# A hybrid SSD, GLA and attention layer step: loading each weight block in two steps

## The chip, the cores and the metric

One core of a Trainium2 chip runs the whole program in one launch. The metric is the device time of one execution in microseconds, as the median of several runs; lower is better.

## The reference, cut to what matters

The reference runs two layers over a context sequence of 128 tokens and a latent sequence of 2048 tokens. Each layer normalises its input, projects it with one wide matrix, runs three groups of heads on the result and projects back:

```python
shift, scale, gate = modulation(c, w_ada, b_ada)
h = rms_norm(x, norm_w) * (1 + scale[:, None]) + shift[:, None]
z, xbc, dt, gq, gk, gv, gg, glr, aq, ak, av, ag = split_proj(h @ w_in)
y_ssd, _ = ssd_branch(z, xbc, dt, conv_w, conv_b, a_log, dt_bias, d_skip, ssd_norm_w, ssd_h0)
y_gla, _ = gla_branch(gq, gk, gv, gg, glr, gk_up, gk_b, gla_norm_w, gla_s0)
y_att = latent_attention(qh, kh, vh, k_ctx, v_ctx, sink) * jax.nn.silu(ag)
y = jnp.concatenate([y_ssd, y_gla, y_att], axis=-1) @ w_out
return x + gate[:, None] * y
```

`w_in` is 1024 x 3120 and `w_out` 1024 x 1024 for each layer, in float32.

## The kernel before, in words

**Tiles and stages.** The tokens are 17 tiles of 128 rows: 16 latent tiles and one context tile (CT). The normalised input of all tiles stays on the chip, transposed, as two float16 halves (a value and what rounding left over) in the tile `HT`. Each layer runs in stages: GLA's chunked scan in groups of two tiles (A), attention tile by tile (T) with the outputs of GLA between, the SSD's convolution and scan (S), and the output projection (O), which also normalises the next layer's input. Every projection is the function `prod` (L276 to L282): 24 float16 matmuls that add three products of halves for each of the eight blocks of 128 input columns.

**Loading weights.** A block of 256 columns of `w_in` or `w_out` is 1 MB in float32 and goes to one of nine slots (ring at L227, `slot` at L229). `load_w` (L233 to L271) makes 34 such loads, 17 for each layer. It

- issues the transfer from SyncE's (SP's) queue (L241);
- squares the block on ScalarE (ACT) with a sum along each row into `amx` (L246, or L252 in six pieces for `w_out`); the squares themselves are thrown away into the shared buffer `upper`;
- adds these sums over the partitions with a 128x1 matmul on TensorE (PE), `all_sum` (L219 to L223), whose result is a PSUM tile of tag "m";
- makes a power of two of it in seven small VectorE (DVE) operations (`pow2_scale`, L188 to L204), scales and rounds the block into `upper` on ACT (L257, L263), takes the rest on DVE into the slot (L258, L264) and copies the rounded half from `upper` into the slot (L265).

There is one `upper` for all loads, so the next load's squares wait until L265 has read the one before. The loads of a layer stand in the list `todo` (L292, L293) in the order wqk, wv, wdl, waq, wakv, wag, wgg, wx0 to wx3, wz0, wz1, wo0 to wo3; `upto(n)` makes those up to the n-th. It is called between the stages' steps: three loads at the start of the program; one after each of several GLA groups (L1283, L1285, L1428); at L1357 before GLA's outputs; after the attention tiles 1, 4, 7, 13 and 15 (L1387 to L1389); after the SSD groups 1 to 3 (L1407), and once before the output stage (L1408). The three first loads of layer 1 come during layer 0's output stage (L1422, L1426).

**PSUM.** Its eight banks are given out by tag: "d" has two, "s" four and "m" two (L147). Projections mostly take "d" and "s". "m" serves `all_sum`, `all_max`, transposes, the modulation (L365), GLA's products (L596, L616), attention's values (L892) and the states (L1033).

**The order of the work.** The kernel is written as one long program; a planner, built into the language, orders the instructions of each engine from their places in the program and a plan of when their inputs are ready, so on each engine the order can differ from the text, but each engine runs its own list in order, waiting wherever an input is late.

**Start of the program.** The modulation's rows for the latent tiles go through DRAM (L416, read back by L456). The context tile is transposed by PE (`normalise`, L446); a latent tile is normalised on DVE (L461, L462), split (L463 on ACT, L464 on DVE) and transposed by a DMA (L466). Layer 1's modulation weights come by transfers from GpSimd's (POOL's) queue (L350).

Of the kernel before, what the change touches and what calls it, by code (L numbers as in the profile page):

```python
# [14 lines left out]
AF = mybir.ActivationFunctionType  # L15
ALU = mybir.AluOpType
# [4 lines left out]
P = 128  # L21
# [57 lines left out]
def hybrid_kernel(ctx, tc, a, o):  # L79
# [139 lines left out]
    def all_sum(src):  # L219

        pr = psum()
        T.matmul(pr[:, 0:1], lhsT=ones, rhs=src, start=True, stop=True)
        return pr[:, 0:1]  # L223
# [5 lines left out]
    def slot():  # L229
        ring.append(ring.pop(0))  # L230
        return slots[ring[-1]]

    def load_w(src, l, ranges, name, dst=None, row_scale=None):  # L233
        n = sum(y - x for x, y in ranges)
        raw = slot() if dst is None else dst
        st = view(raw, [P, KB, n])
        w = view(raw, [P, 2, KB, n], F16)
        hi = view(upper, [P, KB, n], F16)
        off = 0
        for x, y in ranges:  # L240
            D.dma_start(st[:, :, off:off + y - x], src[l, :, x:y].rearrange("(k p) c -> p k c", p=P))  # L241
            off += y - x

        amx = sb("wmx", [P, 1])
        if row_scale is None:
            S.activation(hi.bitcast(BF16), st, AF.Square, accum_out=amx)  # L246
        else:

            blocks = [slice(k, k + 1) for k in range(4)] + [slice(4, 6), slice(6, 8)]
            part = sb("wmp", [P, 6])  # L250
            for i, ks in enumerate(blocks):
                S.activation(hi[:, ks].bitcast(BF16), st[:, ks], AF.Square, scale=row_scale[:, i:i + 1], accum_out=part[:, i:i + 1])  # L252
            V.tensor_reduce(amx, part, AX.X, ALU.add)
        c, ci = pow2_scale(all_sum(amx), "w", True)

        if row_scale is None:
            S.activation(hi, st, AF.Copy, scale=c)  # L257
            V.scalar_tensor_tensor(w[:, 0], st, c, hi, ALU.mult, ALU.subtract)  # L258
        else:
            cg = sb("wcg", [P, 6])  # L260
            V.tensor_scalar(cg, row_scale, c, None, ALU.mult)
            for i, ks in enumerate(blocks):
                S.activation(hi[:, ks], st[:, ks], AF.Copy, scale=cg[:, i:i + 1])  # L263
                V.scalar_tensor_tensor(w[:, 0, ks], st[:, ks], cg[:, i:i + 1], hi[:, ks], ALU.mult, ALU.subtract)  # L264
        V.tensor_copy(w[:, 1], hi)  # L265
        inv = sb(name + "i", [P, 1])
        if row_scale is None:
            V.tensor_tensor(inv, ci, hinv[l], ALU.mult)
        else:
            V.tensor_copy(inv, ci)  # L270
        return w[:, ::-1], inv  # L271

    def load_in(l, *ranges, name, dst=None):
        return load_w(a["w_in"], l, ranges, name, dst)
# [210 lines left out]
            s.wg, s.ig = load_in(l, (2064, 2320), name="wgg")  # L485

    def gla_begin(l, s, order):

        s.inc = 0 if order == sorted(order) else 1
        s.order = order  # L490
        s.iq = sb("giq", [P, 1])
        V.tensor_scalar(s.iq, s.iqk, 32.0 ** -0.5, None, ALU.mult)
        s.up = sb("ups", [P, P])
        for d in range(2):
            D.dma_start(s.up[32 * d:32 * d + 16], a["gla_gk_up"][l, d])
            D.dma_start(s.up[32 * d + 16:32 * d + 17], a["gla_gk_b"][l, d:d + 1])

        s.sx, s.dec = k_gla
        V.memset(s.sx[:, 0, 1], 0.0)
        V.memset(s.sx[:, 1, 2], 0.0)  # L500
        s.ent = sb("ent", [P, 4, 64])
        e = 0 if s.inc == 0 else 2 * len(GROUPS[order[0]]) - 1
        D.dma_start(s.ent[:, e], a["state_gla"][0, l, s.inc].rearrange("h k v -> (h k) v"))
        s.lr = [sb("lr", [P, 2, 64]) for i in range(2)]
        for x in s.lr:
            G.memset(x, 1.0)
        s.am = [sb("am", [P, 4, 2, 64]) for i in range(2)]
        s.at = [sb("at", [P, 4, 64]) for i in range(2)]
        for x in s.am:
            G.memset(x, 0.0)  # L510
        dt_raw[l] = k_dtraw
# [150 lines left out]
        D.dma_start(o["new_state_gla"][0, l, 1].rearrange("h k v -> (h k) v"), s.sx[:, 1, 0])  # L662

    def gla_out_begin(l, s):
        s.igh = sb("ggh", [P, 1])
        V.tensor_scalar(s.igh, s.ig, 0.5, None, ALU.mult)
        s.bd = [sb("bd", [P, 2, 2, P]) for i in range(1)]
        for x in s.bd:
            G.memset(x, 0.0)
# [66 lines left out]
            s.wg, s.ig = load_in(l, (2864, 3120), name="wag")  # L736

    def att_begin(l, s):
        s.sca, s.nw, s.sink, s.vc, s.kct, s.isc = k_att
        s.igh = sb("aigh", [P, 1])  # L740
        s.pts = [[sb(f"pts{kv}", [P, 1024]) for kv in range(2)], halves(slot())]
        V.tensor_scalar(s.igh, s.ig, 0.5, None, ALU.mult)
        for hh in range(6):
            src = a["attn_q_norm"] if hh < 4 else a["attn_k_norm"]
            D.dma_start(s.nw[:, hh], src[l:l + 1, :].to_broadcast([P, 64]))
        D.dma_start(s.sink, a["attn_sink"][l:l + 1, :].to_broadcast([P, 4]))

        kc = sb("asq", [P, 2, 64])
        D.dma_start(kc, a["cache_k"][0, l])
        vc = sb("qkx", [P, P])  # L750
        D.dma_start(vc, a["cache_v"][0, l].rearrange("s h d -> s (h d)"))

        mw = sb("mw", [P, 2])
        V.tensor_reduce(mw[:, 0:1], s.nw[:, 0], AX.X, ALU.max, apply_absolute_value=True)
        V.tensor_reduce(mw[:, 1:2], s.nw[:, 4], AX.X, ALU.max, apply_absolute_value=True)
        V.tensor_scalar(mw, mw, 12.0, None, ALU.mult)
        mk = sb("tmx", [P, 1])
        V.tensor_reduce(mk, kc, AX.XY, ALU.max, apply_absolute_value=True)
        V.tensor_tensor(mw[:, 1:2], mw[:, 1:2], all_max(mk), ALU.max)
        cq, iq = pow2_scale(mw[:, 0:1], "t")  # L760
        ck, ik = pow2_scale(mw[:, 1:2], "t")
        V.tensor_scalar(s.nw[:, 0:4], s.nw[:, 0:4], cq, None, ALU.mult)
        V.tensor_scalar(s.nw[:, 4:6], s.nw[:, 4:6], ck, None, ALU.mult)
        V.tensor_copy(s.isc[:, 1:2], ik)
        V.scalar_tensor_tensor(s.isc[:, 0:1], iq, 0.125, ik, ALU.mult, ALU.mult)
        V.tensor_scalar(kc, kc, ck, None, ALU.mult)
        x16 = sb("x16", [P, 1024], F16)
        split_keys(x16, kc)
        D.dma_start_transpose(out=s.kct, in_=x16[:, 512:1024])

        mv = sb("tmx", [P, 1])
        V.tensor_reduce(mv, vc, AX.X, ALU.max, apply_absolute_value=True)
        bv = sb("abv", [P, 1])
        V.tensor_scalar(bv, s.ikv, hnorm[l], None, ALU.mult)
        V.tensor_tensor(bv, bv, all_max(mv), ALU.max)
        cv, iv = pow2_scale(bv, "t")
        s.vs, s.igv = s.sca[:, 0:1], s.sca[:, 1:2]
        V.tensor_tensor(s.vs, s.ikv, cv, ALU.mult)
        V.tensor_tensor(s.igv, s.igh, iv, ALU.mult)
        split(s.vc, vc, cv)  # L780
        s.qt, s.kt, s.v, s.pt, s.rl = {}, {}, {}, {}, {}
# [216 lines left out]
        s.w.append(w)  # L998

    def ssd_begin(l, s):  # L1000
        s.Z = arena(sb("SS", [P, where["SS"][2]]))

        s.sl, s.at = [[s.Z([P, P], BF16) for d in range(2)] for i in range(2)], [s.Z([P, P], BF16) for i in range(2)]
        s.sr = [s.Z([P, 8, P], BF16) for i in range(2)]
        for x in s.at:
            G.memset(x, 1.0)

        for x in s.sl:
            for d in range(2):
                G.memset(x[d], 0.0)  # L1010
                G.memset(x[d][64 * d:64 * d + 32], 1.0)
        D.dma_start(s.dsk, a["ssd_d"][l:l + 1].to_broadcast([P, 8]))
        s.wx, s.cw = [], []
        for j in range(4):
            w, iw = s.w[j]
            s.wx.append(w)

            cw = s.Z([P, 5, 2])
            V.tensor_scalar(cw, vec[l][:, 0:40].rearrange("p (j b) -> p j b", b=8)[:, :, 2 * j:2 * j + 2], iw, 0.5, ALU.mult, ALU.mult)
            s.cw.append(cw)  # L1020
        s.cbias = s.Z([P, 8])
        V.tensor_scalar(s.cbias, vec[l][:, 40:48], 0.5, None, ALU.mult)
        s.h, s.accs = {}, {}
        for d in range(2):
            ssd_enter(l, s, d, "s0")
# [132 lines left out]


    def out_begin(l, s):  # L1160
        s.wz, s.izh = [], []
        for j in range(2):
            w, iz = s.w[4 + j]
            izh = sb(f"izh{j}", [P, 1])
            V.tensor_scalar(izh, iz, 0.5, None, ALU.mult)
            s.wz.append(w)
            s.izh.append(izh)
        s.wo, s.io = zip(*s.w[6:10])

        s.rows = halves(slot())  # L1170
# [119 lines left out]
    def loads(l, gla, att, ssd):  # L1290
# [2 lines left out]
        todo += [(ssd_load, ssd, i) for i in range(10)]  # L1293

        def upto(n):
            while len(todo) > 17 - n:
                f, s, i = todo.pop(0)
                f(l, s, i)
# [165 lines left out]
```

## Time and profile before

| | |
|---|---|
| median of three runs | 2300.2 us (2296.73 to 2302.02) |
| profiled execution | 2304.28 us |
| its span | 2302.5 us, 53686 instructions |
| mean granted TensorE clock | 0.959 of full speed |

The span is the time from the first to the last instruction of the profiled execution; times of day in the rows below are microseconds from its start. PE is a matmul, PEld its weight load.

### The profile page before, as it was taken

The numbers are of one execution on the slowest core, as the hardware profiler recorded it, in microseconds if no ns is written. First come the engines' busy times: TensorE is split into PE (matmuls) and PEld (weight loads), VectorE is DVE, ScalarE is ACT, GpSimd is POOL, SyncE is SP. The second block draws the span as 40 slices with busy tenths as digits, with TensorE's granted clock in tenths as the row PEclk, the third lists the DMA queues.
The fourth block names the chain that finished last, engine by engine and source line by source line (L and its number), as shares of the span: only waits on it lengthen the run. The fifth ranks groups of instructions, "written<-read, shape, count | busy, mean of one in ns | idle before, by whom it ended". The sixth has DMA issues, their size and how long they took to land. (4 is left out here: it accounts for less than half of the span.)

```text
span 2302.5 us, 53686 instructions
## 1 busy us (share of the span) xinstructions
PE 2080.7 (90%) x21228; PEld 1750.4 (76%) x21245; DVE 1628.4 (71%) x4088; ACT 992.4 (43%) x2185; POOL 878.6 (38%) x918
## 2 busy tenths in 40 slices
PE   2596888999899899998999999899999999989998
PEld 0364767778688788887888887777888778878887
DVE  2465768887599988666665657898779988854442
ACT  2333554665444434433333554666563433422221
POOL 0010015556434354544442003566643344444442
PEclk6797979999899999999999999999999999999999
DMA  8687434576710112676667123556751101265553
GB/s 298 165 263 158 121 103 92 124 154 143 168 58 33 38 38 91 183 199 163 168 160 201 41 69 100 122 125 149 160 139 43 38 33 42 81 182 164 154 146 96
DMA packets 486352, 288.01 MB, mean 125 GB/s; under 512 B 354344, under 2 KB 447924, under 8 KB 483796
## 3 DMA queue, kind: packets, MB, share of 16 engines
q1 hardware_dynamic: 483796, 271.99, 45.4%
q0 software_dynamic: 2304, 12.58, 1.8%
q8 instruction: 167, 2.74, 0.5%
q14 instruction: 85, 0.70, 0.1%
HBM read 141.11 MB, written 64.93 MB: 89 GB/s over the span
## 5 line engine op out<-in xcount | busy, mean ns | idle before, releaser
L281 PEld LDWEIGHTS <-HT 128*128 128x128 f16 x6528 | 583.6, 99 | 128.3 <-issue 50.7
L281 PEld LDWEIGHTS <-slot 128*128 128x128 f16 x4320 | 402.3, 98 | 107.5 <-issue 31.3
L281 PE MATMUL pd<-slot,HT 128*128 128x256 f16 x3456 | 430.8, 279 | 10.3 <-DVE work L728 8.0
L281 PE MATMUL pd<-slot,work 128*128 128x256 f16 x3264 | 366.8, 273 | 8.0 <-DMA work<-work 7.7
L281 PEld LDWEIGHTS <-work 128*128 128x128 f16 x3264 | 319.6, 98 | 50.2 <-DMA work<-work 9.1
L281 PE MATMUL pd<-HT,slot 128*128 128x260 f16 (+3 forms) x2592 | 318.0, 270 | 15.7 <-DMA HT<-work 14.5
L281 PE MATMUL ps<-HT,slot 128*128 128x260 f16 (+1 forms) x1728 | 202.8, 272 | 4.8 <-DVE work L1059 4.8
L281 PE MATMUL ps<-slot,HT 128*128 128x256 f16 x1440 | 169.6, 275 | 17.7 <-ACT work L1192 17.7
L1252 POOL TENSOR_TENSOR work<-work 128x512 f32<-128x512 f32 x68 | 90.1, 1325 | 185.5 <-DVE work L1251 156.2
L875 POOL TENSOR_TENSOR work<-work 128x512 f16<-128x512 f32 (+2 forms) x102 | 123.3, 1211 | 86.0 <-ACT work L874 70.8
L1059 DVE SCALAR_TENSOR_TENSOR work<-ps,work 128x256 f32<-128x256 f32 (+1 forms) x288 | 133.3, 464 | 9.1 <-ACT work L1057 4.6
L793 POOL TENSOR_TENSOR work<-work 128x384 f32<-128x384 f32 x34 | 30.2, 889 | 276.1 <-ACT work L789 174.4
L1059 DVE SCALAR_TENSOR_TENSOR work<-pd,work 128x256 f32<-128x256 f32 (+1 forms) x288 | 132.1, 463 | 3.0 <-ACT work L1057 0.3
L872 ACT ACTIVATE work<-ps,nm,K 128x512 f32<-128x512 f32 (+2 forms) x136 | 100.6, 742 | 54.7 <-DVE nm L864 39.3
L1120 POOL TENSOR_TENSOR work<-work 128x512 f32<-128x512 f32 x68 | 72.3, 1068 | 112.6 <-ACT work L1079 67.6
L1061 ACT ACTIVATE work<-work 128x256 f32<-128x256 f32 (+1 forms) x144 | 58.1, 403 | 123.4 <-DVE work L1059 87.4
L854 PEld LDWEIGHTS <-work 128*128 128x128 f16 x1008 | 71.5, 99 | 41.8 <-issue 34.4
L1218 ACT ACTIVATE work<-work 128x512 bf16<-128x512 f32 x68 | 42.7, 628 | 138.3 <-DMA work<-work 75.5
L1093 POOL TENSOR_TENSOR work<-K,work 128x512 bf16<-128x512 bf16 x68 | 73.5, 1081 | 73.7 <-PE ps L1104 63.8
L874 ACT CAST work<-work 128x512 f16<-128x512 f32 (+2 forms) x136 | 78.0, 586 | 52.3 <-DMA slot<-work 31.4
L281 PE MATMUL pm<-slot,HT 128*128 128x256 f16 x816 | 96.1, 275 | 1.6 <-DVE work L907 1.3
L854 PE MATMUL ps<-work 128*128 128x128 f16 x752 | 76.2, 223 | 21.8 <-DMA work<-work 21.8
(375 smaller groups left out, 4029.2 us busy)
## 6 DMA issues: line engine op xcount, KB each, us to landing
slot<-in_w_in_dram SPq DMA_DIRECT2D x24, 1024.0 KB
ymix<-work SPq DMA_DIRECT2D x68, 128.0 KB
yacc<-work SPq DMA_DIRECT2D x34, 256.0 KB
work<-ymix SPq DMA_DIRECT2D x34, 256.0 KB
work<-yacc SPq DMA_DIRECT2D x34, 256.0 KB
x<-work SPq DMA_DIRECT2D x17, 512.0 KB
work<-x SPq DMA_DIRECT2D x17, 512.0 KB
out_dram<-work SPq DMA_DIRECT2D x17, 512.0 KB
```

The costliest lines, as they stand in the source:

```text
L281: T.matmul(out, lhsT=lhs(i, k), rhs=rhs(j, k), start=(n == 0), stop=(n == 3 * KB - 1))
L793: G.tensor_tensor(sq, x, x, ALU.mult)
L854: T.matmul(ps[:, bs], lhsT=s.qt[t][:, 2 * gg + kv], rhs=kt[:, 2 * kv + j], start=(j == 0), stop=(j == 1 and mk is None))
L872: S.activation(pr, sc[hh][:, :nb * P], AF.Exp, scale=s.isc[:, 0:1], bias=nm[:, hh:hh + 1], accum_out=ls[:, hh:hh + 1])
L874: S.copy(p16[:, 0], pr)
L875: (G if hh else V).tensor_tensor(p16[:, 1], pr, p16[:, 0], ALU.subtract)
L1059: V.scalar_tensor_tensor(acc[:, jj, :W], pp[:, q:q + W], s.cw[j][:, q, jj:jj + 1], acc[:, jj, :W], ALU.mult, ALU.add)
L1061: S.activation(th[:, :W], acc[:, jj, :W], AF.Tanh)
L1093: G.tensor_tensor(sr[:, j:j + 4], oh[:, j:j + 4].unsqueeze(2).to_broadcast([P, 4, P]), at.unsqueeze(1).to_broadcast([P, 4, P]), ALU.mult)
L1120: G.tensor_tensor(xw, x, bc8(s.wst[:, t, 8 * d:8 * d + 8]), ALU.mult)
L1218: S.activation(junk, ym[:, 512 * i:512 * i + 512], AF.Square, accum_out=ss[:, i:i + 1])
L1252: G.tensor_tensor(xs[:, js], xs[:, js], tm, ALU.add)
```

## The change

`load_w` now ends after the squares. Everything from the sum on goes into a function `finish` that is put into the list `half`. `finish_loads` runs what is in the list. It is called at the start of each call of `upto`, ahead of the loads that this call makes, and at the start of every stage (`gla_begin`, `gla_out_begin`, `att_begin`, `ssd_begin`, `out_begin`). Nothing is computed differently.

```diff
+    half = []
+
     def load_w(src, l, ranges, name, dst=None, row_scale=None):
...
             V.tensor_reduce(amx, part, AX.X, ALU.add)
-        c, ci = pow2_scale(all_sum(amx), "w", True)
-
-        if row_scale is None:
-            S.activation(hi, st, AF.Copy, scale=c)
-            V.scalar_tensor_tensor(w[:, 0], st, c, hi, ALU.mult, ALU.subtract)
...
-        V.tensor_copy(w[:, 1], hi)
         inv = sb(name + "i", [P, 1])
...
+        def finish():
+            c, ci = pow2_scale(all_sum(amx), "w", True)
+
+            if row_scale is None:
+                S.activation(hi, st, AF.Copy, scale=c)
+                V.scalar_tensor_tensor(w[:, 0], st, c, hi, ALU.mult, ALU.subtract)
...
+            V.tensor_copy(w[:, 1], hi)
...
+        half.append(finish)
         return w[:, ::-1], inv
+
+    def finish_loads():
+        while half:
+            half.pop(0)()
...
     def gla_begin(l, s, order):
+        finish_loads()
...
     def gla_out_begin(l, s):
+        finish_loads()
...
     def att_begin(l, s):
+        finish_loads()
...
     def ssd_begin(l, s):
+        finish_loads()
...
     def out_begin(l, s):
+        finish_loads()
...
         def upto(n):
+            finish_loads()
             while len(todo) > 17 - n:
```

## Rows read from the trace of the kernel before

**Rows 1.** The page, part 1: busy time, share of the span and instructions of each engine.
```profile
PE 2080.7 (90%) x21228; PEld 1750.4 (76%) x21245; DVE 1628.4 (71%) x4088; ACT 992.4 (43%) x2185; POOL 878.6 (38%) x918
```
**Rows 2.** Stretches: length, busy PE, PEld, DVE, ACT, POOL, then PEclk, DMA share, GB/s.
```profile
36.00:60.00 24.00, 2.00 (x9) 1.83 (x10) 10.60 (x39) 8.81 (x10) 1.11 (x2) 0.50 0.72 239
...
294.00:345.00 51.00, 41.98 (x553) 33.12 (x550) 33.57 (x125) 26.00 (x67) 7.19 (x10) 0.73 0.40 106
...
631.00:672.00 41.00, 40.33 (x360) 34.29 (x361) 38.68 (x116) 19.90 (x50) 11.66 (x12) 0.95 0.24 75
```
**Rows 3.** PE's waits from 0 to 97 us: us in total, times, longest.
```profile
PE pm L222 <- ACT upper L246: 20.7, 2, 10.5
PE pd L281 <- DMA HT<-work: 14.5, 1, 14.5
...
PE pm L446 <- DVE wcl L191: 4.3, 1, 4.3
```
**Rows 4.** Timeline, 46 to 97 us: start, length, engine, line, tiles, count [idle before <-releaser].
```profile
46.34 1.91 ACT L246 ACTIVATE upper<-slot 128x2048 bf16<-128x2048 f32 x1 [3.19 <-issue]
...
48.40 0.58 PE L222 MATMUL pm<-wmx,K 128*128 128x1 f32 x2 [10.46 <-ACT upper L246]
...
57.69 0.68 DVE L265 COPY slot<-upper 128x2048 f16<-128x2048 f16 x1
...
58.53 0.52 ACT L246 ACTIVATE upper<-K 128x384 bf16<-128x384 f32 x1 [6.32 <-DVE mw L756]
...
59.20 0.58 PE L222 MATMUL pm<-wmx,K 128*128 128x1 f32 x2 [10.22 <-ACT upper L246]
...
62.31 1.28 DVE L461 SCALAR_TENSOR_TENSOR slot<-slot,rs,slot 128x1024 f32<-128x1024 f32 x1 [3.49 <-DMA slot<-mrow]
...
71.51 1.03 ACT L463 CAST work<-slot 128x1024 f16<-128x1024 f32 x1
...
81.66 3.85 SPq L466 DMA_TRANSPOSE HT<-work  x1
...
83.00 0.58 POOL L350 DMA_DIRECT2D slot<-in_w_ada_dram  x1
...
96.84 1.01 PE L281 MATMUL pd<-HT,slot 128*128 128x256 f16 x4 [14.48 <-DMA HT<-work]
```
**Rows 5.** Timeline: the squares of the load waq and its sum.
```profile
76.86 1.91 ACT L246 ACTIVATE upper<-slot 128x2048 bf16<-128x2048 f32 x1 [2.33 <-issue]
...
246.22 0.28 PE L222 MATMUL pm<-wmx,K 128*128 128x1 f32 x2
```
**Rows 6.** Line 222 after 97 us: its matmuls, and who waited for it.
```profile
L222 PE MATMUL pm<-wmx,K x62: 164/250/351, 246.2 to 2007.9; 128*128 128x1 f32 x62
...
  DVE wcl L191: 4.2, 4
```
**Rows 7.** Timeline, layer 0, from GLA to attention: the load wgg, then wx0.
```profile
294.65 0.28 PE L222 MATMUL pm<-wmx,K 128*128 128x1 f32 x2
...
305.03 0.69 DVE L265 COPY slot<-upper 128x2048 f16<-128x2048 f16 x1
...
306.02 1.91 ACT L246 ACTIVATE upper<-slot 128x2048 bf16<-128x2048 f32 x1
```
**Rows 8.** Timeline, from attention to SSD: the load wz1 of layer 0, of layer 1.
```profile
630.73 0.42 PE L222 MATMUL pm<-wmx,K 128*128 128x1 f32 x2
...
636.65 0.60 PE L1033 MATMUL pm<-K,work 128*128 128x128 f32 x4
...
646.13 0.69 DVE L265 COPY slot<-upper 128x2048 f16<-128x2048 f16 x1
...
1703.95 0.28 PE L222 MATMUL pm<-wmx,K 128*128 128x1 f32 x2
...
1710.24 0.60 PE L1033 MATMUL pm<-K,work 128*128 128x128 f32 x4
...
1712.30 0.68 DVE L265 COPY slot<-upper 128x2048 f16<-128x2048 f16 x1
```

More of the change, by code (lines that the diff above doesn't have):

```diff
@@ L253, in load_w @@
             V.tensor_reduce(amx, part, AX.X, ALU.add)
-        c, ci = pow2_scale(all_sum(amx), "w", True)
-        if row_scale is None:
-            S.activation(hi, st, AF.Copy, scale=c)
-            V.scalar_tensor_tensor(w[:, 0], st, c, hi, ALU.mult, ALU.subtract)
[L259 to L264, printed above, removed]
-        V.tensor_copy(w[:, 1], hi)
-        inv = sb(name + "i", [P, 1])
[L267 to L270, printed above, removed]
+        inv = sb(name + "i", [P, 1])
+        def finish():
[3 more added lines that the diff above has]
+                V.scalar_tensor_tensor(w[:, 0], st, c, hi, ALU.mult, ALU.subtract)
+            else:
+                cg = sb("wcg", [P, 6])
+                V.tensor_scalar(cg, row_scale, c, None, ALU.mult)
+                for i, ks in enumerate(blocks):
+                    S.activation(hi[:, ks], st[:, ks], AF.Copy, scale=cg[:, i:i + 1])
+                    V.scalar_tensor_tensor(w[:, 0, ks], st[:, ks], cg[:, i:i + 1], hi[:, ks], ALU.mult, ALU.subtract)
+            V.tensor_copy(w[:, 1], hi)
+            if row_scale is None:
+                V.tensor_tensor(inv, ci, hinv[l], ALU.mult)
+            else:
+                V.tensor_copy(inv, ci)
+        half.append(finish)
         return w[:, ::-1], inv
+    def finish_loads():
+        while half:
+            half.pop(0)()
     def load_in(l, *ranges, name, dst=None):
```

## The prediction

> **What bounds the kernel now.** I read the busy line first [rows 1]: TensorE (PE) is busy for 90% of the span, so a change pays only where PE waits. Then the table by stretch [rows 2]: PE works almost without a break in the stretch at 631 us, but from 36 to 60 us it does 2.00 us of work in 24 us. Then PE's waits in the first 97 us [rows 3]: the longest group, 20.7 us in two waits, is the little matmul of `all_sum` (L222) waiting for a load's squares on ScalarE (ACT, L246). The timeline [rows 4] shows why the second one is long. The squares of `wv` run at 46.34, its sum at 48.40. The next load, `wdl`, cannot square until `wv`'s split has been copied out of the shared buffer `upper` (57.69 + 0.68 = 58.37), so its squares start at 58.53 and its sum at 59.20; PE has stood for 10.22 us, with the transposes of the context tile and the modulation matmuls behind it. The transposes' second half then waits 4.3 us more for the sum's PSUM buffer [rows 3].
>
> Later loads look different. The squares of `waq` start at 76.86, yet its sum runs at 246.22 [rows 5]: the sum takes a buffer of the PSUM tag "m", two of them handed out in program order, and has to wait for its turn. After 97 us no PE wait ends on squares: the 62 sum matmuls there (two to a sum) are listed with no idle time before them, and DVE waited 4.2 us for them in all [rows 6]. So outside the start the loads cost PE nothing now that the change could take away.
>
> **The change part by part.** *Work.* Nothing is added or removed: the same 34 transfers, squares, sums and splits, in the same forms. 24 of the 34 sums and splits move to a later place in the program; wx0, wz1 and wo3 of both layers, wgg of layer 0 and the first three loads stay, because a stage begins or the next load follows at once. The transfers' DMA issues on SP keep their place and slot, so no transfer is moved past another by the text; what the planner makes of that is a rival. The moved split costs its own instructions in either place; what covers it is PE work of other stages, and where this cover is thin I price it below.
>
> *The start.* In the new order the squares of `wv` and of `wdl` both come before either split. Those of `wdl` can follow at 46.34 + 1.91 + 0.15 = 48.4 (0.15 for the read of the accumulator is an estimate, from the gap to the sum at 48.40), take 0.52 + 0.15 [rows 4], and its sum can run at about 49.1 instead of 59.20. That takes away the 10.22 us wait [rows 4]; `wv`'s sum still waits 10.46 us, since its squares still need `wqk`'s split. What is late next? The latent tiles. Their normalisation needs the modulation rows, whose transfer from DRAM lets L461 begin at 62.31 [rows 4], and this transfer hangs on SP's queue, not on the sums. Two L461 of 1.28 us and a second step of about the same length put the first tile's rounding (L463) at 62.31 + 3 x 1.28 = 66.1, where it ran at 71.51: 5.4 us are free for certain kinds of order only, namely if ACT is no longer held by the late transposes. So the start's gain lies between 5.4 (the latent tiles set the pace) and 10.2 (the whole PE wait is moved forward). As bounds I keep 0 below (the transposing transfer L466, issued at 81.66, lands as late as before, at PE's 96.84) and 10.2 + 4.3 = 14.5 above (the wait for the buffer goes as well). I take the middle of 5.4 and 10.2, 7.8 us, for neither chain is shown to be last in the new order.
>
> *That transposing transfer.* PE's 14.48 us wait ends when it lands, 15.2 us after its issue, with a weight transfer issued by POOL at 83.00 under way [rows 4]. The Trainium skill, "DMA: Bandwidth & Descriptors", section "Latency and other measured facts", gives a transposing DMA 261 GB/s; for these 512 KB that is an estimate of 2.0 us. The trace does not agree for this one. By the page the sum would be 13 us better if the new order kept the two apart.
>
> *Layer 0, GLA to attention.* `wag` is now finished after group step 7, `wgg` is asked for there too, and its stage finishes it on the spot. Two splits stand in a row where one stood: the sum at 294.65, the split out of `upper` by 305.03 + 0.69 = 305.7, then squares of 1.91 + 0.15, then the second sum at 307.8 [rows 7]. All users of tag "m" behind it, the four small matmuls of `att_begin` and the last groups' state products among them, come up to 307.8 - 294.65 = 13.2 us later. Ends: 0 if the projections, which use another tag, fill PE, and 13.2 if they don't. PE is idle for 51 - 41.98 = 9.0 of 51 us there [rows 2], so it is partly bound by such chains; I charge this idle share, 18%, of 13.2: 2.3 us.
>
> *Attention to SSD, both layers.* The same with `wz0` and `wz1`. Layer 0: first sum 630.73, split out by 646.8, squares, second sum at 648.9, while the next user of "m" (L1033) ran at 636.65: 12.3 us later. Layer 1: 1703.95, 1713.0, 1715.1 against 1710.24: 4.9 us [rows 8]. Ends again 0 and the full 12.3 and 4.9. Here the convolution's products, on other tags, fill PE (40.33 of 41 us) and VectorE (DVE) is busy 38.68 [rows 2], so I charge PE's idle share, 1.6%, of both: 0.3 us. If that cover ran out, the full figures would be due.
>
> *The moved splits elsewhere.* They come one load's step later, which is still ahead of the stage that uses the weights; I take 0, hidden behind the products that fill PE, and at either end their price is inside the bounds above.
>
> **Sum.** -7.8 + 2.3 + 0.3 = -5.2 us. Against the profiled execution's own 2304.3 us (span 2302.5) that is 2299.1; this execution is 4.1 us above the median of 2300.2. From the median the forecast is 2295.0 us. A measurement of this kernel can tell about 0.2%, 4.6 us, from no change.
>
> **Rivals.**
> *Swallowed at the start* (no change): PE is free at 49 but the latent tiles' rows and the transposing transfer come when they came, and PE waits longer at 96.84 instead. For it: that wait is the second longest group of the first 97 us, and ends on a DMA. Against: L463 visibly stood behind ACT work that comes earlier. Gain 0, edges 2.6: 2302.8.
> *The buffers of tag "m" at the edges* (slower): the second sum of a pair holds up everything that takes an "m" buffer. Its full price is 13.2 + 12.3 + 4.9 = 30.4; at half of it and with the start's 7.8 the time is 2300.2 + 15.2 - 7.8 = 2307.6. It decides as soon as PE stands for more than 7.8 + 4.6 = 12.4 us longer at the three edges. For it: the 9.0 us of idle PE in the stretch from 294. Against: 40.33 of 41 us busy from 631.
> *The transposing transfer set free*: in a new order it no longer meets POOL's weight transfer, and lands 13 us sooner, whatever becomes of the sums: 2300.2 - 5.2 - 13 = 2282. For it: the rate that the page beside it above gives; against it: the weight transfers of layer 1 move forward with PE's modulation matmuls, so they probably meet again.
> *It does not do what it says*: the order on each engine is laid out from a plan of the whole program, in which squares already run early and sums late [rows 5]; the text may move and the order hardly: 2300.
>
> **How the numbers follow.** Forecast case 0.38 (its own range 2289 to 2299), swallowed 0.28, edges 0.23, set free 0.05, no effect 0.06. Faster by over 0.2%: 0.38 + 0.05 = 0.43; within: 0.28 + 0.06 = 0.34; slower: 0.23. The range goes from 2286 (the start's bound of 14.5 off the median) to 2309 (edges at half price, and 1.4 for a smaller gain); outside are the transfer set free and the edges at full price, 2300.2 + 30.4 - 7.8 = 2322.8.
>
> **What would show it.** Right: `wdl`'s squares follow `wv`'s at once, no 10 us wait before its sum, the context tile's transposes near 50 us, the first latent group's products several microseconds before 96.84, and this lead still there at 246 us. The pairs of sums at the three edges should lie 13 to 18 us apart with PE busy between. Wrong: the lead gone at 97 us, idle PE between the pairs, or a difference that arises in stretches where no load is.

## The result, and the profile after

| | before | after |
|---|---|---|
| median | 2287.7 us (11 runs, 2278.7 to 2302.1) | 2312.8 us (11 runs, 2306.3 to 2324.2) |
| profiled execution, its span | 2304.3 us, 2302.5 us | 2311.0 us, 2309.2 us |
| mean granted clock in it | 0.959 | 0.958 |

The change makes the kernel **slower by 1.0%**: ratio 1.0103, 95% interval 1.0080 to 1.0126. The forecast was 5 us faster, with 2309 us as the upper end of its range. The three runs that it started from had a median of 2300.2 us, 12.5 above that of the eleven: executions of this kernel lie as far apart as 2275.0 and 2303.4 us (23 runs on one chip). So the two profiles alone (+6.7 us) understate the loss, and stretches are set against a second profile of the kernel before (2295.2 us, span 2293.4) as well.

PE's busy time in the profile after, to set beside [rows 1]:

```profile
PE 2098.0 (91%) x21231; PEld 1760.4 (76%) x21245; DVE 1632.0 (71%) x4088; ACT 994.6 (43%) x2185; POOL 883.2 (38%) x918
```

PE does the same work and is busy for 17 us more than in the first profile, so the loss isn't idle time alone.

**The start went as forecast.** The timeline of the changed kernel, 45 to 90 us (start, length, engine, line, tiles, count, [idle before and what ended it]):

```profile
45.70 1.91 ACT L249 ACTIVATE upper<-slot 128x2048 bf16<-128x2048 f32 x1 [3.19 <-issue]
...
47.73 0.52 ACT L249 ACTIVATE upper<-K 128x384 bf16<-128x384 f32 x1
...
47.75 1.24 PE L222 MATMUL pm<-wmx,K 128*128 128x1 f32 x4 [10.50 <-ACT upper L249]
...
48.85 1.95 PE L457 MATMUL pm<-K,slot 128*128 128x128 f32 x8
...
69.02 1.04 ACT L474 CAST work<-slot 128x1024 f16<-128x1024 f32 x1 [6.43 <-DVE slot L473]
...
78.92 5.96 SPq L477 DMA_TRANSPOSE HT<-work  x1
...
86.98 5.71 PE L292 MATMUL pd<-HT,slot 128*128 128x256 f16 x34 [6.51 <-DMA HT<-work]
```

`wdl`'s squares follow `wv`'s at once, and the second wait of some 10 us on squares is gone (in [rows 4] it stood ahead of 59.20). The group of [rows 3] has one wait left, and the one for the transposing transfer is under half as long (us in total, times, longest):

```profile
PE pm L222 <- ACT upper L249: 10.5, 1, 10.5
PE pd L292 <- DMA HT<-work: 6.5, 1, 6.5
```

The context tile's transposes run at 48.85 us and not at 59.64. The transposing transfer lands at 86.98 and not at 96.84. GLA's group 7 begins at 264.2 us where it began at 283.7, a lead of 19.6 us.

**And it was lost in later stretches.** The next rows cut the programs at the same instructions (the counts differ where the new order moves work over a cut, by 53 matmuls in the first line): the first line is from GLA's group 7 to the first transposes of the scan's tile 1 (layer 0), the second is GLA of layer 1 up to its attention tile 3, the third is layer 1 from attention tile 15 to the scan's tile 15, the fourth is layer 0's scan from tile 7 to tile 15. Columns: stretch, length, busy PE, PEld, DVE, ACT, POOL with their instructions, then granted clock, DMA share, GB/s. The kernel before, second profile:

```profile
286.82:683.77 396.95, 353.70 (x3948) 299.85 (x3948) 311.93 (x835) 217.74 (x514) 188.48 (x211) 0.96 0.53 124
1244.49:1429.27 184.78, 179.32 (x2938) 150.38 (x2937) 116.49 (x372) 97.02 (x225) 17.14 (x20) 0.98 0.30 81
1639.48:1991.40 351.92, 338.14 (x2952) 287.89 (x2957) 304.81 (x785) 159.20 (x359) 154.85 (x155) 0.99 0.26 71
790.57:924.57 134.00, 133.78 (x1077) 114.74 (x1080) 114.89 (x292) 53.15 (x116) 59.77 (x55) 1.00 0.21 67
```

The changed kernel:

```profile
264.19:674.29 410.10, 359.72 (x3895) 303.71 (x3895) 315.84 (x831) 220.83 (x513) 193.55 (x211) 0.93 0.53 120
1240.51:1435.83 195.32, 184.51 (x2941) 152.73 (x2939) 119.32 (x377) 99.58 (x229) 17.23 (x22) 0.96 0.29 78
1643.76:2007.09 363.33, 341.89 (x2956) 289.60 (x2960) 310.28 (x795) 161.01 (x360) 154.24 (x155) 0.99 0.25 69
779.95:919.35 139.40, 136.77 (x1079) 115.40 (x1082) 121.27 (x307) 55.60 (x122) 59.27 (x54) 0.99 0.20 65
```

Read the length first, then PE's busy time and the clock. In GLA of layer 1 PE does the same matmuls (some 2940), but takes 10.5 us longer: half of it is idle (5.5 against 10.8 us, length less busy), half is the clock (0.98 against 0.96, so the same matmuls are busy for 5.2 us more). From attention tile 15 of layer 1 on it is 11.4 us, of which 7.7 is idle. In the last line PE before had 0.2 us of idle time in 134; with the split of `wo2` moved into it, DVE is busy 6.4 us longer and PE stands 2.6 us. The stretches between these lines change little: the scan of layer 0 from tile 1 to tile 7 is 1.1 us shorter, layer 1's attention from tile 3 to tile 15 is 2.3 us shorter, and from tile 15 of layer 0's scan to GLA of layer 1 it is 1.2 us longer. With the 22.6 us that the changed kernel is ahead of the second profile at group 7, and 0.1 us at the end, all of this adds up to the difference of the two spans, 15.8 us.

### The profile page after: what moved, and what is told of

The parts are those of the page before. It is cut to its first block, busy times and chain, and to the rows that moved or that the text cites. A ratio compares the mean times of both kernels' runs of the same rounds, so it can differ in the third digit from the quotient of the medians.

```text
span 2309.2 us, 53664 instructions
## 1 busy us (share of the span) xinstructions
PE 2098.0 (91%) x21231; PEld 1760.4 (76%) x21245; DVE 1632.0 (71%) x4088; ACT 994.6 (43%) x2185; POOL 883.2 (38%) x918
## 4 chain that ended last, share of the span: by engine, by line
PE 35%; DVE 30%; DMA 13%; ACT 7%; issue 7%; POOL 5%; SPq 2%; POOLq 0%; DVEq 0%; ACTq 0%
PE pd L292 18%; PE ps L292 7%; DVE work L1074 4%; DMA work<-work 3%; DVE mx L871 2%; DMA HT<-work 2%; DMA slot<-work 2%; PE ps L1138 1%; PE ps L1159 1%; DMA x<-work 1%; DVE slot L264 1%; DVE work L1077 1%; DVE ps L1120 1%; DMA slot<-in_x_sample_dram 1%; DVE slot L270 1%
## 5 line engine op out<-in xcount | busy, mean ns | idle before, releaser
L292 PE MATMUL pd<-HT,slot 128*128 128x260 f16 (+3 forms) x2592 | 322.7, 273 | 14.9 <-DMA HT<-work 6.5
```

Source lines behind the costliest of these rows:

```text
L292: T.matmul(out, lhsT=lhs(i, k), rhs=rhs(j, k), start=(n == 0), stop=(n == 3 * KB - 1))
```

## The experiments

**The kernel before, once more, and the two halves.** In the changed kernel one condition decides which loads are finished at once. This is the start alone; the start undone has the condition without `not`, and the third kernel has `name[:2] in ("wx", "wz")`:

```diff
         half.append(finish)
+        if not (l == 0 and name in ("wqk", "wv", "wdl")):
+            finish_loads()
         return w[:, ::-1], inv
```

> The kernel before, profiled once more, since its profile lies at the slow end of its own runs (2304.3 us against a median of 2287.7 us). Every theory expects the same order on each engine and about 2288 us. Where this profile differs by stage from the first one (I expect it in the first 250 us, where PE waits of 10 to 15 us end on transfers) is what runs differ in by themselves, and isn't to be explained by the change.

Measured: 2295.2 us. The stretches from the output stage of layer 0 to layer 1's scan agree with the first profile within 1.5 us each; the ones up to 685 us differ by up to 5.

> Two steps for the first three loads of layer 0 alone, every other load finished at once. Theory A (the loss comes from the later loads: their splits come late and stand together at the ends of the stages): the start's gain is left alone, 2287.7 - 8 to 11 = 2277 to 2280 us. Theory B (the loss comes from the planner, which lays the whole program out anew as soon as one load moves): the start's gain shows at 50 us, but stages in which no load has moved differ by several us either way, and the time lies anywhere from 2280 to 2310 us. Theory C (the start's gain is swallowed): 2288 us.

> The changed kernel with the first three loads of layer 0 finished at once; all others in two steps. Theory A: the loss without the gain, 2312.8 + 8 to 11 = 2321 to 2324 us. Theory B: not additive, between 2295 and 2320 us. Theory C: the same as the changed kernel, 2313 us.

> The changed kernel with wx0 to wx3, wz0 and wz1 of both layers finished at once, as before; the others in two steps. Theory A in its form for the attention stage (wx3, wz0 and wz1 are split together between 586 and 645 us, and PE stands or works slower there: +9.3 us from attention tile 7 to scan tile 1 of layer 0, some 4 to 8 us in layer 1): 2312.8 - 13 to 17 = 2296 to 2300 us, and the stretch from attention tile 7 to the first scan returns to that of before. Theory D (the loss lies with layer 1's wdl and its GLA loads, +11 us): 2313 us less at most 5. Theory B: 2300 to 2315 us with no stage that returns.

Measured: the start alone 2289.4 us, ratio 1.0006 (0.9981 to 1.0032); the start undone 2311.8 us, 1.0098 (1.0059 to 1.0136); `wx` and `wz` at once 2300.5 us, 1.0046 (1.0023 to 1.0070). So the start's part is worth nothing that can be measured, in either direction: theory C holds in time, although the profile of the start alone shows the lead (group 7 at 264.4 us). And theory A's share for `wx` and `wz` came back, 12.3 us; the stretch that its expectation named, from attention tile 7 to the first scan of layer 0, is 84.5 us before (second profile), 94.8 in the changed kernel and 87.2 here.

The start-only kernel also shows that an edit can change a stage that it doesn't touch. Its loads of layer 1 are those of before, yet GLA of layer 1 takes 189.5 us and not 184.8 (stretch as in the second lines above):

```profile
1226.40:1415.90 189.50, 179.82 (x2938) 149.64 (x2937) 117.54 (x372) 97.93 (x225) 17.45 (x20) 0.98 0.29 78
```

PE's order in it is another one, while the two profiles of the kernel before have the same order from end to end. One exchange can be read off. In the kernel before, 29 matmuls of a projection (L281) stand ahead of a GLA matmul (L589) that needs a result of DVE's:

```profile
1345.40 3.33 PE L281 MATMUL pd<-HT,slot 128*128 128x256 f16 x29
1348.65 0.53 PE L589 MATMUL ps<-work 32*64 32x64 f32 x32
```

In the start-only kernel the GLA matmul (now L603) stands ahead of them, and PE waits for DVE:

```profile
1327.02 0.61 PE L294 MATMUL pd<-K,HT 128*128 128x48 f16 x18
1329.69 0.54 PE L603 MATMUL ps<-work 32*64 32x64 f32 x32 [2.05 <-DVE work L592]
```

The changed kernel has the same exchange, and a wait of 2.0 us with it (below).

**Each of the other parts alone**, with the conditions `name[:2] not in ("wx", "wz")`, `name[:2] != "wo"`, `name not in ("waq", "wakv", "wag", "wgg")`, and `l == 0 or name not in ("wqk", "wv", "wdl")`.

> Two steps for wx0 to wx3, wz0 and wz1 of both layers alone; all else finished at once. Theory A (each part has its own price, where its loads are, and the prices add up): the changed kernel with these six at once was 12.3 us faster (2300.5 against 2312.8), so alone they cost about +12: 2300 us, lost between attention tile 7 and the scan's tile 1 and nowhere before. Theory B (the planner's new layout of everything is what costs): a difference from -5 to +10 us, spread over stages without these loads.

> Two steps for wo0 to wo3 of both layers alone. Theory A: the stretch from scan tile 7 to scan tile 15 is 134.0 us in every kernel with these at once and 139.4 to 139.8 us in every one with them in two steps, in both layers; if that is not taken back by the stretch before it, +5.5 in each layer: about 2299 us. Rival: the work only moves past the milestone (what is late after tile 7 was early before it): 2288 us, and the whole stretch from the first scan to tile 15 is unchanged.

> Two steps for waq, wakv, wag and wgg of both layers alone. Theory A: the stretches from GLA's group 7 to attention tile 7 of layer 0 and from GLA's first groups to attention tile 7 of layer 1 carry what is left of the loss, some +5 to +9 us: 2293 to 2297 us. Theory E (the edge of GLA and attention costs what the forecast charged): +2.3 us, 2290 us.

> Two steps for wqk, wv and wdl of layer 1 alone; wdl is then finished at the start of GLA of layer 1 (1233 us in the changed kernel) and not 64 us earlier. Theory A: PE stands at most for the chain from the sum to the split of this small block, about 7 us, so 2288 to 2295 us, at the start of layer 1. Theory F (PE has other work there): 2288 us. With the three others this should add up to the changed kernel's +25 us and the start's gain of 8 to 11 us, if theory A holds; if the four add up to under 15 us, the rest is what the parts do to each other.

| in two steps | median, us | ratio (95% interval) |
|---|---|---|
| start | 2289.4 | 1.0006 (0.9981 to 1.0032) |
| wx, wz | 2321.6 | 1.0124 (1.0075 to 1.0173) |
| wo | 2302.5 | 1.0044 (1.0011 to 1.0076) |
| waq, wakv, wag, wgg | 2302.2 | 1.0050 (1.0024 to 1.0076) |
| wqk, wv, wdl of layer 1 | 2302.9 | 1.0050 (1.0022 to 1.0077) |
| all of these | 2312.8 | 1.0103 (1.0080 to 1.0126) |

Every part but the start costs. They don't add up: 0.06 + 1.24 + 0.44 + 0.50 + 0.50 = 2.7%, the whole change 1.0%. `wx` and `wz` alone cost about as much as the change that holds them (the two intervals overlap), and the expectations for the last two parts, 2297 and 2295 us at most, were too low. Theory A in its simple form, a price for each part in its own place that adds up, is out. Its local reading stands in part for `wo` alone, where PE's order outside the scans is that of before: the scan from tile 7 to tile 15 is 139.6 us (134.0 before) in layer 0, and DVE has 6.7 us more to do in it.

```profile
793.64:933.24 139.60, 136.94 (x1082) 115.38 (x1082) 121.61 (x307) 55.63 (x122) 59.23 (x54) 0.99 0.19 65
```

The rival in that run's expectation holds in part as well: some of this work only moves past tile 7. From tile 1 to tile 7 the scan is shorter, by 0.9 us in layer 0 and by 4.0 in layer 1, where 5.5 are lost after tile 7. From tile 1 to tile 15 both layers together lose 6.2 us against the second profile and 3.5 against the first.

**The start by itself**, with everything after layer 0's GLA groups left out:

```diff
-    for l in range(L):
+    for l in range(0):
         gla, att, ssd = state[l]
```

> The kernel before, cut off after layer 0's GLA groups (all of attention, the SSD, the output stage and layer 1 are left out, and the outputs are not written). The full kernel's profiles reach this point at about 310 us. This isolates the start: in five profiles with the old start GLA's group 7 begins at 277.6 to 291.3 us, in three with the new one at 264.2 to 266.0 us, yet the kernel with the new start alone takes the same time as before (ratio 1.0006). Theory G (the start's gain is real and is lost again later): this kernel is slower than the next one by 12 to 20 us. Theory H (the gain shows in profiled executions only): the two agree within 5 us in their medians.

> The changed kernel, cut off at the same point. Theory G: 12 to 20 us below the cut kernel before. Theory H: within 5 us of it.

Measured: 312.0 us before, 330.2 us changed; the fastest run of the changed one (323.7 us) is slower than the slowest of the other (317.0). Both theories are wrong: cut off here, the change is slower. Its lead is there (transposes at 47.5 against 59.5 us, GLA's first group 8 us earlier) and gone by 150 us. PE's waits after 96 us, changed kernel, cut off (waiting line, releaser: us, times, longest):

```profile
PE pd L292 <- DVE var L442: 12.6, 1, 12.6
PE ps L557 <- DVE work L553: 8.8, 3, 4.3
PE pm L376 <- DMA slot<-in_w_ada_dram: 7.7, 3, 6.1
```

The wait at the top, on a variance of a latent tile's normalisation, is in no profile of the full kernels here; the planner had laid out these shorter programs in another way, also ahead of the cut (PE's order departs from that of the full kernel at 127 us before, and at 60 us in the changed one). So this pair doesn't show what becomes of the lead in the full kernel. It does show that a lead at the start is only as good as the order behind it.

**Other orders of the same work.** If the loss were the price of the moved splits, it should show under any order of the rest. First the planner's other mode:

```diff
-    with tile.TileContext(nc, schedule_with_timeline_sim=True) as tc:
+    with tile.TileContext(nc) as tc:
```

> The kernel before, its order laid out by the planner without the option that times the instructions in a simulated timeline. It sets the base for the next run; I expect 2290 to 2350 us.

> The changed kernel under that other layout. Theory A (the loss comes from splits that are moved into stretches where PE has no slack, whoever lays out the order): the scan's stretch from tile 7 to tile 15 is some 5 us longer in each layer, the stretch from attention tile 15 to the first scan some 8 to 10 us, and the time lies 15 to 30 us above the run before. Theory B (the loss is an accident of one layout): within 8 us of the run before, or faster.

Measured: 2448.3 and 2444.8 us; the means differ by -0.9 us, give or take 6.7 (two standard errors). The sums move as they did (that of `wx3` of layer 0 from 506.1 to 623.0 us, in the changed kernel of this study from 503.3 to 586.1), the transposes lead by 10.1 us, and nothing is lost. But this order has more slack: PE is idle for 56 us in the two long stretches of layer 1 (second and third line above), where the kernel before is for 19. So two orders with little slack:

```diff
-            for _ in range(4):
+            for _ in range(3):
                 step(we)
```

and, for the second, the sum's PSUM buffer (in `all_sum`):

```diff
-        pr = psum()
+        pr = psum(None, "s")
```

> The kernel before with all_sum's PSUM tile taken from tag s (four buffers) and not m (two). It is the base for the next run, with an order of its own; 2280 to 2310 us.

> The changed kernel with all_sum on tag s. If the buffers of tag m cause the loss (the forecast's rival): at most 5 us above the run before, and the stretch from attention tile 15 to the first scan no longer 8 to 10 us longer. If the moved splits as such cost (theory A): 15 to 30 us above it. If it is the accident of one layout (theory B): anything from -10 to +30, in other stretches than before.

> The kernel before with three and not four steps of the next tile's attention weights ahead of each tile's values: the same work, another order in the attention and scan stages. Base for the next run; 2275 to 2310 us.

> The changed kernel with the same three steps. Theory A: 15 to 30 us above the run before, again with 8 to 10 us in the stretch from attention tile 15 to the first scan, some 5 us in the scan after tile 7 and 5 to 10 us in GLA of layer 1. Theory B: the difference in the attention and scan stages is another one, by 10 us or more, and that in GLA of layer 1, whose order hardly changes, stays at about +10 us.

| order | before, us | changed, us | difference of the means |
|---|---|---|---|
| as it is | 2287.7 | 2312.8 | 22.6 +- 6.3 us |
| sums on tag s | 2275.6 | 2284.5 | 10.0 +- 6.9 us |
| three steps | 2298.0 | 2301.8 | 3.9 +- 4.8 us |
| planner's other mode | 2448.3 | 2444.8 | -0.9 +- 6.7 us |

The same edit costs 23 us, 10 us and, in the last two orders, nothing that can be told from zero. Theory B holds for the size. It isn't all chance either. With three steps the two stretches of layer 1 lose what they lost before, 13.1 us (184.0 to 197.2) and 10.9 us (352.3 to 363.1), and the new order wins part of it back elsewhere (7.1 us in layer 1's attention between the two). In the first of these stretches PE's order is the same as in the pair without the edit, before and after: the same exchange of orders costs the same again. With the sums on tag s, the same two stretches lose next to nothing, 189.7 to 187.9 us and 349.4 to 351.4 us, but the first is already 4.9 us longer in its base than in the kernel before. In both of these orders most or all of the 29 projection matmuls (23 before, 29 changed) stand ahead of the GLA matmul, and neither has the wait of 2.0 us. Changed kernels, second and third stretch, with three steps and then with the sums on s:

```profile
1234.48:1431.63 197.15, 186.15 (x2940) 153.86 (x2939) 119.31 (x376) 99.45 (x227) 17.23 (x22) 0.95 0.29 76
1635.89:1999.04 363.15, 341.80 (x2933) 287.92 (x2938) 311.74 (x797) 162.01 (x364) 158.89 (x153) 0.98 0.24 68
```

```profile
1249.44:1437.33 187.89, 179.00 (x2959) 150.41 (x2959) 122.39 (x380) 98.63 (x229) 16.88 (x20) 0.98 0.30 82
1642.30:1993.67 351.37, 337.33 (x2923) 285.44 (x2928) 309.13 (x794) 159.90 (x361) 155.59 (x153) 1.00 0.24 70
```

That spoke for the forecast's rival of the tag "m" buffers, so two last runs tested it: the start's part with the sums on s, and the kernel before with `all_max` moved to tag s as well (the same edit at its two tiles).

> Sums on tag s and two steps for the first three loads of layer 0 alone; everything else at once. If the start's gain holds once the later loss on tag m is gone: 8 to 11 us below the kernel before with the sums on s, 2265 to 2268 us. If it is swallowed before the first layer ends: 2274 to 2280 us, and the stretch from GLA's group 7 to scan tile 1 is longer by what the start had won.

> The kernel before with the sums and all_max (its transpose and its small product) on tag s. If tag m is what holds PE up: 2268 to 2275 us, a little below the kernel before with the sums alone on s (2275.6). If that one's gain was the luck of one layout: anywhere from 2275 to 2300 us.

Measured: 2275.3 us, ratio to the kernel before 0.9944 (0.9921 to 0.9968), and 2290.6 us, 0.9991 (0.9973 to 1.0010). The start's part makes no difference here (1.8 +- 7.3 us against the kernel before with the sums on s, from two chips), but it had nothing to remove. With the sums on tag s alone, PE's waits on squares in the first 97 us, 20.7 us in [rows 3], are down to this:

```profile
PE ps L222 <- ACT upper L246: 1.1, 1, 1.1
```

And taking more off tag m gives back all that the sums had won, though that kernel has no such wait at all. So tag m as the cause is not shown; each of these edits draws a new order, and the orders that the planner makes in its first mode for the loads of before differ by about 1%. The version that beats both kernels is the kernel before with the sums on tag s, 2275.6 us, ratio 0.9903 (0.9875 to 0.9932, six runs), with the warning that one small edit more took it away.

A last rival is that the order before was a lucky one, so that any edit costs. The runs speak against it: the four kernels that move no later load and differ in their order all the same (the start alone, three steps, the sums on s, the sums and `all_max` on s) have ratios of 1.0006, 1.0011, 0.9903 and 0.9991. The seven that move some of the later loads, and change nothing else, have 1.0044 to 1.0124.

## Why the prediction was wrong

**The step that failed is "The moved splits elsewhere", taken at 0.** 24 sums and splits move to a later place, and I hid them "behind the products that fill PE". Measured together, with the start undone, they cost 0.98%, some 23 us; each group of them, alone, costs 0.4 to 1.2%. Two things were wrong in it. The first is the cover. That PE is busy for 98% of a stretch [rows 2] is no cover for work on ACT and DVE. In the scan of layer 0 after tile 7, DVE has 6.4 us more to do, and PE stands for 2.6 us where it stood for 0.2, and 2.2 of the 2.6 are waits for results of DVE. The second is the premise that the rest stands still. I had the planner only as a rival in which the text moves "and the order hardly"; the other case, that a moved load lays out stages anew which hold no load, had no chance and no price, and it decides between +23 us and nothing.

**Layer 1's GLA** shows how a stretch without slack loses. `wdl`'s sum and split come at 1233 to 1241 us where they came at 1164 to 1172 (second profile), and the four loads behind it follow later. PE's waits in this stretch (second lines above), before (second profile), then after; the first rows of each list:

```profile
PE ps L854 <- DMA work<-work: 2.1, 1, 2.1
PE pd L281 <- DVE work L535: 0.8, 1, 0.8
PE pd L281 <- ACT work L806: 0.8, 1, 0.8
```

```profile
PE pm L628 <- ACT work L610: 3.3, 2, 3.1
PE pm L906 <- DMA slot<-work: 2.2, 1, 2.2
PE ps L601 <- DVE work L590: 2.0, 1, 2.0
```

The longest wait of after, in its timeline:

```profile
1385.45 6.25 SPq L611 DMA_DIRECT2D oacc<-work  x2
...
1390.97 0.37 ACT L610 COPY work<-pm 128x256 f32<-128x256 f32 x1 [5.21 <-DMA oacc<-work]
...
1391.40 0.86 PE L628 MATMUL pm<-work 64*32 64x64 f32 x24 [3.12 <-ACT work L610]
```

GLA's state product (L628) needs an "m" buffer, which ACT is to empty (L610), which waits until the store of the tile before has read its buffer, while the DMA engines are 92% busy with a weight block (last section). Before, ACT waits for that store too (8.0 us in all, 7.5 after), but PE has none of its waits there. The wait of 2.0 us (L601, for DVE) is the one that the 29 projection matmuls covered before: here too they no longer stand ahead. The same two gaps, 2.0 and 3.1 us, stand in the kernel with three steps.

**The start** (-7.8): right at 50 us (an 11 us lead, 10.2 was the wait to be removed, `wdl`'s squares at 47.73 where I had 48.4). The rounding of the first latent tile gains only 2.5 us (69.02 against 71.51), as its rows are late at 64.12. When PE begins to wait for the transposing transfer, the lead is down to 1.9 us (80.47 against 82.36). It is back to 9.9 us at the end of that wait, because the wait shrank from 14.5 to 6.5. The other 10 us up to group 7 come above all from another wait, PE's for layer 1's modulation weights (90 to 330 us; before, first profile, and after):

```profile
PE pm L365 <- DMA slot<-in_w_ada_dram: 14.0, 4, 10.2
PE pm L376 <- DMA slot<-in_w_ada_dram: 1.5, 2, 0.9
```

No term of the forecast had this wait, and it differs between executions: with the sums on tag m it is 4.1 to 17.8 us in eight profiles with the old start and 1.5 to 3.9 in four with the new one. Of these twelve and the four with the sums on s, the nine profiled executions with 9 us or more of it lie 7.5 us above the median of their kernel on average, the other seven at 0.0. So part of the lead belongs to the executions that were profiled: the profile of the start alone ends 12.0 us ahead of the second one of the kernel before, while their medians are the same. In time the start is worth nothing, alone and undone: measured alone it is +1.4 us, between -4 and +7, so the -7.8 was wrong as well. The rival "swallowed" named the outcome, not the place: it had PE waiting longer for that transfer. Where the lead goes is shown in part, 4.7 us in layer 1's GLA; how large it is in an execution at the median isn't shown, and executions with the old start reach group 7 anywhere from 269.7 to 291.3 us.

**GLA to attention in layer 0** (+2.3): the pair of sums lies 12.3 us apart, and PE is busy for all of it, so this edge costs nothing. **Attention to SSD** (+0.3): the pairs lie 22.2 and 14.9 us apart, 13 to 18 being foreseen. The three pairs in the changed kernel, columns as in the stretches above:

```profile
272.63:284.94 12.31, 12.31 (x182) 10.32 (x177) 9.08 (x29) 6.42 (x9) 0.00 (x0) 1.00 0.58 139
613.03:635.24 22.21, 18.02 (x152) 14.06 (x151) 21.62 (x69) 11.54 (x23) 8.40 (x7) 0.85 0.14 40
1704.76:1719.63 14.87, 14.07 (x148) 12.05 (x147) 14.43 (x47) 8.36 (x16) 4.70 (x7) 1.00 0.33 108
```

PE stands 4.2 and 0.8 us between the last two, while DVE is busy 97% of both. I charged these edges by PE's idle share, 1.6%, though [rows 2] also had DVE busy for 38.68 of 41 us: the engine that the moved work runs on was nearly full. And it was not a pair but three: `wx3`, due one step later, joins `wz0` and `wz1`. The instructions on `upper` from attention's end of layer 0 to the scan, before (second profile, from 495 us) and after (from 580 us); the columns are line, count, duration in ns, first and last start:

```profile
L257 ACT ACTIVATE upper<-slot,wc x3: 1992/2002/2010, 506.2 to 637.4; 128x2048 f16<-128x2048 f32 x3
L258 DVE SCALAR_TENSOR_TENSOR slot<-slot,wc,upper x3: 2341/2346/2351, 509.6 to 639.4; 128x2048 f16<-128x2048 f32 x3
```

```profile
L263 ACT ACTIVATE upper<-slot,wc x3: 1991/2002/2003, 592.9 to 639.4; 128x2048 f16<-128x2048 f32 x3
L264 DVE SCALAR_TENSOR_TENSOR slot<-slot,wc,upper x3: 2351/2352/2352, 595.0 to 641.4; 128x2048 f16<-128x2048 f32 x3
```

Three splits whose starts were spread over 131 us now start within 47. The rival of the "m" buffers, the one on the slower side, put the price at the edges at 15 us; the three edges cost 5.0 us of PE between the sums (0 + 4.2 + 0.8), so at these edges it is not what made the kernel slower. That the two stretches of layer 1 lose next to nothing with the sums on tag s is an indication for it, but the base of that pair is slower in one of them already, and the last run speaks against it.

**The two small rivals.** The transposing transfer was not set free: in the changed kernel it takes 8.1 us from issue (78.92) to PE's start (86.98), in the second profile of the kernel before 16.4 us (82.92 to 99.31). The Trainium skill, "DMA: Bandwidth & Descriptors", section "Latency and other measured facts", by whose rate it would take an estimated 2.0 us, is met by neither. And the change did what it says: the sums stand later in PE's list wherever the text put them later, `wx3`'s of layer 0 by 83 us.

**What is shown and what isn't.** Shown: every moved group but the start costs; the prices don't add; the size of the whole hangs on the order that the planner makes; stretches with no slack lose in idle time and clock together; in layer 1's GLA one exchange in the order makes PE wait 2.0 us. Not shown: what in the new order makes the rest of the ten us of each stretch, and how much of the start's lead an execution at the median has.

## What to carry to other kernels

Where a planner orders the program, an edit of a few lines can be a new draw of the whole order. Compare lists of instructions in stages that the edit doesn't touch, and repeat the edit under a second and a third order before you believe its price. A moved split is charged by the slack of the engines that run it and of what waits for them, not by PE's idle share alone; and before a few us are forecast, take more than three runs and two profiles of the base.

## What the runs showed of the hardware

A short wait can cost more than its own length. In the changed kernel the stretches behind the waits of 2.0 and 3.1 us in layer 1's GLA run without a break, but at half the granted clock, 1.2 GHz, where it was 2.4 GHz ahead of them:

```profile
1352.00:1358.00 6.00, 6.00 (x151) 5.13 (x146) 2.51 (x8) 4.51 (x14) 0.00 (x0) 1.00 0.15 48
1360.60:1367.30 6.70, 6.70 (x86) 4.85 (x73) 3.67 (x14) 1.43 (x3) 0.00 (x0) 0.50 0.25 71
1384.00:1388.00 4.00, 4.00 (x90) 3.38 (x89) 2.10 (x11) 1.49 (x4) 0.00 (x0) 1.00 0.92 267
1391.40:1398.00 6.60, 6.60 (x57) 4.48 (x58) 3.45 (x10) 2.87 (x9) 0.00 (x0) 0.50 0.20 62
```

Not every such wait does it. Behind the start-only kernel's wait of 2.05 us in the same place the clock stays at 2.4 GHz. From this wait on both kernels run the same 181 matmuls in the same order, the changed one first:

```profile
1360.21:1372.17 11.96, 11.96 (x181) 9.09 (x181) 4.20 (x15) 2.73 (x7) 0.00 (x0) 0.71 0.19 54
1329.69:1338.77 9.08, 9.08 (x181) 7.27 (x182) 4.01 (x15) 2.63 (x7) 0.00 (x0) 1.00 0.23 67
```

So a wait of 2.0 us was followed by a loss of 2.9 us at the lower clock in one kernel, and by none in the other. And one transposing transfer of 512 KB, in the same place, held PE for 8.5 to 17.2 us in eight profiles with the old start and the sums on tag m, and for 6.0 to 8.2 us in four with the new one.
